# A gated linear unit that takes its columns as they lie in SBUF instead of in token order

## The chip, the cores and the metric

The kernel runs on one core of one Trainium2 chip. The metric is device time in microseconds (us) of one execution; the lower the better. The core has five engines that matter here: TensorE (PE in the profile, with its weight loads as PEld), VectorE (DVE), ScalarE (ACT), GpSimd (POOL) and the queue engine SyncE (SP), which issues most transfers. Each runs its own instructions in order and waits on semaphores for the others.

## The reference

One layer of a hybrid decoder over 2064 tokens (16 learned ones ahead of 2048) with 1024 features: a gated short convolution beside a diagonal state-space model (SSM), an output projection, then a gated MLP. The part that matters is the end of the SSM's branch, over 512 features:

```python
y = y.reshape(bsz, seq_len, D_SSM)
g = jax.nn.gelu(y)
out = g * jax.nn.sigmoid(g @ w_glu.astype(f32))
...
mixed = jnp.concatenate([rms_norm(conv_out, gain_conv_out[i]),
                         rms_norm(ssm_out, gain_ssm_out[i])], axis=-1)
h = h + mixed @ w_out[i].astype(h.dtype)
```

So g (512 features by 2064 tokens) is multiplied by a 512x512 weight, passed through a sigmoid, and multiplied onto itself. The columns of that product are independent of each other: any order of tokens gives the same result as long as the sigmoid meets its own column of g.

## The kernel before

Features lie on the 128 partitions, tokens on the free axis. All products are split in two parts to keep single precision: a matrix is written as hi + lo, and each output gets three matmuls, hi x hi, hi x lo and lo x hi (`product`, lines 128 to 142; the second operand is the one with 344 columns). Weights are loaded by SyncE (L119), their hi part is made by ScalarE and their lo part by VectorE (`parts`, L248 and L109), a few ahead of use by the class `Stream`. VectorE's two-operand operations all go through one helper, so that they all show as L109; one tells them apart by the names of the tiles.

The SSM works on chunks of 8 tokens and writes its result g to DRAM by position in the chunk. `load_glu` (L1012) reads it back as the tile `gt` of shape [128, 4, 8, 258]: feature group k, position j in the chunk (8), chunk c (258). Token number is 8c + j, so tokens that follow each other lie 258 elements apart in `gt`.

The tokens are handled in three blocks b of 688 columns, each in two halves c of 344 columns, which are 43 chunks of 8. Four steps use `gt`:

- `prep_glu` (L1016) makes the hi and lo parts of g for a block: `gh` on ScalarE (L1021), `gl` on VectorE (L1022, shown as L109). Six of each.
- `glu_block` (L1072) does the four products `pg` of a block, 24 matmuls each, with the weights `wh_g` and `wl_g`; then ScalarE's sigmoid into `sg` (L1079) and VectorE's gate product, `gt` times `sg`, in place (L1081, shown as L109). Twelve of each.
- `prep_ssm` (L1026) takes the RMS norm of the result: squares `sq_ms` (L164), sums on VectorE and, over partitions, on TensorE (`st_ms`, L188), the inverse root on GpSimd, its diagonal `dg_ms` (L203), a broadcast on TensorE (`sb_ms`, L208), the scaled `t_ms` (L1033), and its parts `h_ms` (L1038) and `l_ms`. It writes these in token order with the same helper `tokens`.
- `out_block` and `OutProj` multiply these by the output weight (`po`), adding the convolution's part, which `conv_part` has computed and kept for block 0 (`pk`, `kp`, L1064). The convolution's branch goes through the same steps as `prep_ssm` under the names `x_mc`, `sq_mc`, `st_mc`, `sb_mc`, `t_mc`, `h_mc` and `l_mc`, all unbroken.

The helper `tokens` turns a tile that lies in token order into a view by position: `(c j) -> j c`. Read or written through it, neighbours in the inner loop lie 8 elements apart.

Around the GLU the order of work is that in which the code is written, with `prep.step` letting the preparations for later blocks go forward between the products: `conv_part(0)`, `glu_block(0)`, `glu_block(1)`, `glu_block(2)`, `out_block(0)`, and so on. A tile scheduler then puts each engine's instructions in a fixed order; buffers of each pool go round, so that a load or a split waits for the last reader of its buffer.

Of the kernel before, what the change touches and what calls it, by code (L numbers as in the profile page):

```python
# [14 lines left out]
AF = mybir.ActivationFunctionType  # L15
ALU = mybir.AluOpType
# [6 lines left out]
NJ = 8  # L23
# [34 lines left out]
def layer_kernel(ctx, tc, xq, pk, w_in, w_glu, w_out, w_up, w_down, ssm_s, ssm_m, y):  # L58
    nc = tc.nc
    V, S, T, G = nc.vector, nc.scalar, nc.tensor, nc.gpsimd  # L60
# [34 lines left out]
    def mm_tile(name):  # L95
        return ps_mm.tile([P, 2, 512], F32, tag="mm", name=name)
# [5 lines left out]
    def f32(ap):  # L102
        return ap.bitcast(F32)

    def two(ap):
        return ap.rearrange("p (c t) -> p c t", c=2)

    def tt(out, a, b, op):
        V.tensor_tensor(out, a, b, op=op)  # L109

    def mul(out, a, b):
        tt(out, a, b, ALU.mult)
# [15 lines left out]
    def product(ps, w, rhs, nk, by_chunk=False, ks=None):  # L128

        hi, lo = w  # L130
        if by_chunk:
            for c, p in enumerate(ps):
                product([p], w, lambda k, _: rhs(k, c), nk)
            return
        for k in ks or range(nk):
            for c in range(len(ps)):
                xh, xl = rhs(k, c)
                T.matmul(ps[c], hi[:, k, :], xh, start=k == 0, stop=False)  # L138
                T.matmul(ps[c], hi[:, k, :], xl, start=False, stop=False)  # L139
            for c in range(len(ps)):  # L140
                xh, _ = rhs(k, c)
                T.matmul(ps[c], lo[:, k, :], xh, start=False, stop=k == nk - 1)  # L142

    def rhs_of(hs):
        return lambda k, c: (hs[c][k // 4][0][:, k % 4, :], hs[c][k // 4][1][:, k % 4, :])
# [4 lines left out]
    def hl_tile(n, name, pool=None, tag="xhl", bufs=8):  # L150
        return (pool or xf).tile([P, 4, QM], F32R, tag=tag, bufs=bufs, name=name)[:, :, :n]
# [812 lines left out]
    def until(res, n=2):  # L964
        while len(res) < n:
            prep.step()
# [38 lines left out]
    gt = a2.tile([P, 4, NJ, NC], F32, name="gt")  # L1005

    def tokens(a):

        names = "p k (c j) -> p k j c" if len(a.shape) == 3 else "p (c j) -> p j c"
        return a.rearrange(names, j=NJ)  # L1010
# [5 lines left out]
    def prep_glu(b, res, **kw):  # L1016
        for c in range(2):
            hi, lo = hl_tile(QL, f"gh_{b}_{c}", **kw), hl_tile(QL, f"gl_{b}_{c}", **kw)
            c0 = (2 * b + c) * 43
            src = gt[:, :, :, c0 : c0 + 43]  # L1020
            S.activation(tokens(hi), src, AF.Copy)  # L1021
            tt(tokens(lo), src, f32(tokens(hi)), ALU.subtract)  # L1022
            res.append(((hi, lo),))
            yield

# [20 lines left out]
    def ev_tile(name):  # L1046
        return a2.tile([P, B2], F32, tag="ev", bufs=3, name=name)
# [24 lines left out]
    def glu_block(b):  # L1072
        until(hg[b])
        rhs = rhs_of(hg[b])
        for m in range(4):
            ps = mm_tile(f"pg_{b}_{m}")
            product([ps[:, c, :QL] for c in range(2)], stream.take(), rhs, 4, by_chunk=m == 0)
            sg = ev_tile(f"sg_{b}_{m}")
            S.activation(two(sg), ps[:, :, :QL], AF.Sigmoid)  # L1079
            g = gt[:, m, :, b * 86 : b * 86 + 86]  # L1080
            mul(g, g, tokens(sg))  # L1081
            prep.step(2 if b else 1)

    hos = [[] for _ in range(3)]
    load_glu()
    prep.add(prep_glu(0, hg[0]), prep_glu(1, hg[1], **xh2))
    prep.lanes, slack = 1, True
    kept = conv_part(0)
    prep.lanes = 2
    until(hg[0])  # L1090
    prep.add(prep_glu(2, hg[2]))
    glu_block(0)
    until(hg[1])
    prep.add(prep_ssm(0, 0, hos[0]), prep_ssm(0, 1, hos[0]))
    prep.add(prep_conv(1, 0, hoc[1], **xh2), prep_conv(1, 1, hoc[1], **xh2))
    prep.lanes = 3
    glu_block(1)
    until(hg[2])
    glu_block(2)
    prep.lanes = 2  # L1100
    until(hos[0])
# [109 lines left out]
    for i in range(3):  # L1211
        c = C_FW + i * 44 + FT
# [183 lines left out]
    for b in range(3):  # L1396
# [4 lines left out]
        x, act, later = hf[b], {}, deque()  # L1401
# [248 lines left out]
```

## Time and profile before

| | |
|---|---|
| Time, median of 3 runs | 2223.89 us (2220.8 to 2225.02) |
| The profiled execution | 2220.69 us, its span 2218.9 us |
| TensorE busy over the span | 2121.5 us, 96% |
| VectorE busy | 1682.3 us, 76% |
| ScalarE busy | 1102.1 us, 50% |
| First and last start of a GLU matmul | 505.4 and 572.9 us |
| First matmul of the output projection behind it | 573.36 us |

The profile comes from one execution. Its rows give an instruction's engine, line, operation, the tiles it writes and reads, the shape, and a duration; in the order of time a bracket at the end of a row gives how long the engine had been idle before it, and whose work ended that. TensorE's matmuls are pipelined, so that the distance between starts, not the duration shown, is what one costs. The granted clock is TensorE's, as a share of its full speed.

### The profile page before, as it was taken

How to read it: one execution, taken by the hardware profiler on the slowest of the kernel's cores; microseconds unless marked ns; L12 is line 12 of the kernel's file. 1: busy time of each engine (PE TensorE's matmuls, PEld its weight loads, DVE VectorE, ACT ScalarE, POOL GpSimd, SP SyncE). 2: the span in 40 equal slices, each digit the busy share in tenths (PEclk: the TensorE clock that was granted, in tenths of full speed). 3: DMA queues.
4: the chain of work that ended last, by engine and by line, in shares of the span. 5: the costliest groups of instructions: out<-in, count | busy, mean ns of one | idle time of the engine just before them, and what ended most of it. 6: DMA issues, size and time to landing. Idle time of an engine off the chain costs nothing. (4 is left out here: it accounts for less than half of the span.)

```text
span 2218.9 us, 33122 instructions
## 1 busy us (share of the span) xinstructions
PE 2121.5 (96%) x13012; PEld 2061.5 (93%) x13012; DVE 1682.3 (76%) x2507; ACT 1102.1 (50%) x1651; POOL 151.4 (7%) x174
## 2 busy tenths in 40 slices
PE   7997999999899999999999899899999899999996
PEld 7997999998899999999999899899999899999996
DVE  8896499858956887686768869677868868667776
ACT  4135333337423555465556555455556555455555
POOL 0000000000000000100111010100111010110000
PEclk9998999999999999999999999999999999999998
DMA  7376544351576334624555262733555262653463
GB/s 241 108 219 164 145 149 150 108 178 53 162 233 202 134 105 120 142 80 112 129 130 130 91 169 76 211 107 87 139 128 141 82 170 62 158 120 95 101 170 113
DMA packets 170749, 300.28 MB, mean 135 GB/s; under 512 B 32416, under 2 KB 104800, under 8 KB 170464
## 3 DMA queue, kind: packets, MB, share of 16 engines
q1 hardware_dynamic: 149856, 246.41, 35.9%
q0 software_dynamic: 19584, 47.52, 12.6%
q10 hardware_dynamic: 1152, 4.23, 0.5%
q8 instruction: 102, 1.67, 0.3%
q14 instruction: 55, 0.45, 0.1%
HBM read 214.29 MB, written 83.82 MB: 134 GB/s over the span
## 5 line engine op out<-in xcount | busy, mean ns | idle before, releaser
L109 DVE TENSOR_TENSOR wl_up<-wr_up,wh_up 128x1024 fp32r<-128x1024 f32 x198 | 241.6, 1222 | 138.7 <-ACT wh_up L248 132.8
L138 PE MATMUL dn<-ah,wh_dn 128*128 128x344 f32 (+1 forms) x1024 | 327.8, 324 | 10.4 <-ACT ah L248 8.9
L139 PE MATMUL dn<-al,wh_dn 128*128 128x344 f32 (+1 forms) x1024 | 324.7, 320 | 0.4 <-DVE al L109 0.3
L248 ACT ACTIVATE wh_up<-wr_up 128x1024 fp32r<-128x1024 f32 x198 | 209.5, 1059 | 197.3 <-DVE wr_up L109 53.1
L1409 PE MATMUL xy<-h_t,wh_up 128*128 128x344 f32 (+1 forms) x792 | 263.9, 333 | 12.9 <-ACT z L1447 7.9
L1411 PE MATMUL xy<-h_t,wl_up 128*128 128x344 f32 (+1 forms) x792 | 254.0, 321 | 0.0
L1410 PE MATMUL xy<-l_t,wh_up 128*128 128x344 f32 (+1 forms) x792 | 253.7, 320 | 0.0
L142 PE MATMUL dn<-ah,wl_dn 128*128 128x344 f32 (+1 forms) x1024 | 247.3, 320 | 0.0
L138 PEld LDWEIGHTS dn<-ah,wh_dn 128*128 128x128 f32 x1024 | 193.6, 190 | 14.4 <-ACT ah L248 9.7
L1510 POOL DMA_DIRECT2D h_d<-ev x136 | 118.3, 870 | 1233.5 <-ACT ev L1506 1221.0
L139 PEld LDWEIGHTS dn<-al,wh_dn 128*128 128x128 f32 x1024 | 194.2, 190 | 1.8 <-DVE al L109 1.0
L1409 PE MATMUL xy<-h_b,wh_up 128*128 128x344 f32 (+1 forms) x528 | 176.5, 335 | 13.7 <-ACT z L1456 12.2
L1409 PEld LDWEIGHTS xy<-h_t,wh_up 128*128 128x128 f32 x792 | 149.8, 189 | 30.7 <-ACT z L1454 16.4
L142 PEld LDWEIGHTS dn<-ah,wl_dn 128*128 128x128 f32 x1024 | 178.1, 190 | 0.0
L1410 PE MATMUL xy<-l_b,wh_up 128*128 128x344 f32 (+1 forms) x528 | 169.9, 322 | 0.0
L1411 PE MATMUL xy<-h_b,wl_up 128*128 128x344 f32 (+1 forms) x528 | 168.6, 322 | 0.0
L248 ACT ACTIVATE wh_dn<-wr_dn 128x512 fp32r<-128x512 f32 (+1 forms) x144 | 85.5, 594 | 134.7 <-issue 52.5
L1410 PEld LDWEIGHTS xy<-l_t,wh_up 128*128 128x128 f32 x792 | 150.6, 190 | 0.0
L1411 PEld LDWEIGHTS xy<-h_t,wl_up 128*128 128x128 f32 x792 | 150.4, 190 | 0.0
L115 DVE SCALAR_TENSOR_TENSOR g<-z,pv,g 128x688 f32<-128x688 f32 (+1 forms) x132 | 122.3, 927 | 22.9 <-ACT g L1414 22.2
L109 DVE TENSOR_TENSOR wl_dn<-wr_dn,wh_dn 128x512 fp32r<-128x512 f32 (+1 forms) x144 | 92.5, 644 | 58.7 <-ACT wh_dn L248 57.4
L115 DVE SCALAR_TENSOR_TENSOR v<-z,pneg,v 128x688 f32<-128x688 f32 (+1 forms) x132 | 122.4, 928 | 9.4 <-ACT v L1414 8.1
(401 smaller groups left out, 5361.9 us busy)
## 6 DMA issues: line engine op xcount, KB each, us to landing
wr_up<-in_w_up SPq DMA_DIRECT2D x132, 512.0 KB, 5.4
h_d<-ev POOLq DMA_DIRECT2D x88, 344.0 KB, 6.8
wr_dn<-in_w_down SPq DMA_DIRECT2D x96, 256.0 KB, 2.7
wr_cw<-in_w_in SPq DMA_DIRECT2D x36, 512.0 KB, 4.5
h_d<-ev POOLq DMA_DIRECT2D x48, 336.0 KB, 6.6
x_c<-in_xq SPq DMA_DIRECT2D x16, 688.0 KB, 6.4
wr_dn<-in_w_down SPq DMA_DIRECT2D x48, 192.0 KB, 2.3
xr<-in_xq SPq DMA_DIRECT2D x24, 344.0 KB, 3.9
```

Of the source, the lines that this page charges most:

```text
L109: V.tensor_tensor(out, a, b, op=op)
L115: V.scalar_tensor_tensor(out=out, in0=a, scalar=s, in1=b, op0=ALU.mult, op1=ALU.add)
L138: T.matmul(ps[c], hi[:, k, :], xh, start=k == 0, stop=False)
L139: T.matmul(ps[c], hi[:, k, :], xl, start=False, stop=False)
L142: T.matmul(ps[c], lo[:, k, :], xh, start=False, stop=k == nk - 1)
L248: S.activation(hi, t, AF.Copy)
L1409: T.matmul(ps, hi[:, j, :], xh[:, j, :], start=start and j == 0, stop=False, **kw)
L1410: T.matmul(ps, hi[:, j, :], xl[:, j, :], start=False, stop=False, **kw)
L1411: T.matmul(ps, lo[:, j, :], xh[:, j, :], start=False, stop=j == 3, **kw)
L1510: G.dma_start(out=h_d[:, m, s0 : s0 + no], in_=ev, accum_op=ALU.add)
```

## The change

The GLU's product keeps its columns in the order of `gt`, position in the chunk first and then chunk (within each half of 344 columns). Three places follow from it:

- `gh` is written without `tokens`: ScalarE reads `gt` in runs of 43 as before and writes its 344 columns per feature group one after the other.
- `gl` is written, and `gh` read for it, in the same way by VectorE.
- `sg` therefore comes out in that order too. The gate product reads it unbroken, and walks `gt` by half, position and chunk (2 x 8 x 43) instead of by position and chunk (8 x 86).

The matmuls, the sigmoid and `prep_ssm` are the same. Every engine's instructions stand in the same order as before, with the same semaphores waited for; only the access patterns of these 24 instructions differ. Lines behind L1021 move down by one.

```diff
@@ prep_glu
             src = gt[:, :, :, c0 : c0 + 43]
-            S.activation(tokens(hi), src, AF.Copy)
-            tt(tokens(lo), src, f32(tokens(hi)), ALU.subtract)
+            hj, lj = (a.rearrange("p k (j c) -> p k j c", j=NJ) for a in (hi, lo))
+            S.activation(hj, src, AF.Copy)
+            tt(lj, src, f32(hj), ALU.subtract)
             res.append(((hi, lo),))
             yield
@@ glu_block
             S.activation(two(sg), ps[:, :, :QL], AF.Sigmoid)
-            g = gt[:, m, :, b * 86 : b * 86 + 86]
-            mul(g, g, tokens(sg))
+            g = gt[:, m, :, b * 86 : b * 86 + 86].rearrange("p j (c x) -> p c j x", c=2)
+            mul(g, g, two(sg).rearrange("p c (j x) -> p c j x", j=NJ))
             prep.step(2 if b else 1)
```

## The prediction

> **What bounds the kernel now.** First the profiled execution's own time, then the busy time by stretch around the gated linear unit (GLU), from the stretch before it to the first matmul of the output projection that follows it at 573.36 us.
>
> ```profile
> span 2218.9 us, 33122 instructions
> ```
>
> The run took 2220.69 us, 1.8 us more than this span; the median of the three runs shown is 2223.89. The columns below are TensorE matmul, its weight load, VectorE, ScalarE and GpSimd busy time, then TensorE's granted clock and the DMA share.
>
> ```profile
> 480.00:505.50 25.50, 25.50 (x162) 25.50 (x161) 5.75 (x5) 12.30 (x13) 0.00 (x0) 1.00 0.69 228
> 505.50:525.40 19.90, 17.32 (x99) 16.76 (x98) 19.61 (x13) 18.34 (x17) 0.00 (x0) 0.91 0.23 67
> 525.40:549.70 24.30, 21.91 (x122) 21.00 (x120) 18.91 (x34) 9.82 (x14) 3.19 (x3) 0.86 0.22 66
> 549.70:573.36 23.66, 18.69 (x107) 18.23 (x105) 21.09 (x25) 13.18 (x14) 1.16 (x1) 0.86 0.16 53
> ```
>
> Before the GLU, TensorE never pauses: 162 matmuls in 25.5 us, 0.157 us each, clock 1.00. In the three GLU stretches, one for each block of 688 columns, VectorE is busy 19.61 of 19.90, 18.91 of 24.30 and 21.09 of 23.66 us, TensorE has holes and its clock falls to 0.91 and 0.86. So here VectorE, fed by ScalarE, sets the pace, and TensorE, the bound of the program elsewhere, waits. The waits of TensorE from 495 to 600 us name the holes:
>
> ```profile
> PE st_mc L188 <- DVE sq_mc L109: 5.0, 1, 5.0
> PE st_ms L188 <- DVE sq_ms L109: 2.5, 2, 1.8
> PE pg L142 <- DVE wl_g L109: 2.2, 1, 2.2
> PE sb_ms L208 <- DVE dg_ms L203: 0.6, 1, 0.6
> PE pg L138 <- ACT sg L1079: 0.3, 1, 0.3
> ```
>
> Every one ends on a VectorE or ScalarE instruction that is not itself changed, but that stands in its queue behind the changed ones. TensorE's order of time shows what follows a hole:
>
> ```profile
> 505.68 0.32 PE L139 MATMUL pg<-gl,wh_g 128*128 128x344 f32 x1
> 508.24 0.66 PE L142 MATMUL pg<-gh,wl_g 128*128 128x344 f32 x1 [2.24 <-DVE wl_g L109]
> ...
> 511.51 0.32 PE L139 MATMUL pg<-gl,wh_g 128*128 128x344 f32 x1
> ...
> 535.40 1.29 PE L188 MATMUL st_ms<-ones,sq_ms 128*115 128x1 f32 x6 [1.79 <-DVE sq_ms L109]
> 536.55 0.64 PE L138 MATMUL pg<-gh,wh_g 128*128 128x344 f32 x1
> ...
> 542.95 0.32 PE L138 MATMUL pg<-gh,wh_g 128*128 128x344 f32 x1
> ...
> 582.00 0.73 PE L188 MATMUL st_ms<-ones,sq_ms 128*115 128x1 f32 x6 [0.66 <-DVE sq_ms L109]
> ```
>
> From 508.24 to 511.51 there are 11 matmuls: 3.27 us where 11 x 0.157 = 1.73 would do. From 536.55 to 542.95 there is one whole product, 24 matmuls: 6.40 us where 3.77 would do. A hole of about 2 us thus costs 1.5 to 2.6 us more in slow matmuls behind it.
>
> **What each changed instruction costs.** No instruction is added, removed or moved; on every engine and queue the order and the semaphores waited for are those of before. Only access patterns change, on 6 + 6 + 12 instructions. VectorE's groups from 330 to 720 us (last figures: busy us, mean ns), then ScalarE's:
>
> ```profile
> L109 DVE TENSOR_TENSOR gt<-gt,sg 128x688 f32<-128x688 f32 x12 | 18.2, 1517 | 2.5 <-ACT sg L1079 2.5
> L109 DVE TENSOR_TENSOR l_ms<-t_ms,h_ms 128x1376 fp32r<-128x1376 f32 x6 | 17.9, 3008 | 2.8 <-ACT h_ms L1038 2.6
> L109 DVE TENSOR_TENSOR gl<-gt,gh 128x1376 fp32r<-128x1376 f32 x6 | 17.5, 2924 | 10.6 <-ACT gh L1021 10.5
> ...
> L1033 DVE SCALAR_TENSOR_TENSOR t_ms<-gt,pv,rs_ms 128x344 f32<-128x344 f32 x24 | 12.5, 573 | 0.0
> L241 DVE SCALAR_TENSOR_TENSOR t_mc<-x_mc,pv,rs_mc 128x344 f32<-128x344 f32 x24 | 12.3, 584 | 0.0
> ...
> L109 DVE TENSOR_TENSOR l_mc<-t_mc,h_mc 128x1376 fp32r<-128x1376 f32 x6 | 9.4, 1601 | 0.1
> ...
> L109 DVE TENSOR_TENSOR xr<-kp,xr 128x688 f32<-128x688 f32 x8 | 7.1, 882 | 0.0
> ```
>
> ```profile
> L1021 ACT ACTIVATE gh<-gt 128x1376 fp32r<-128x1376 f32 x6 | 17.7, 2950 | 3.4 <-DMA gt<-g_d 3.4
> ...
> L1079 ACT ACTIVATE sg<-pg 128x688 f32<-128x688 f32 x12 | 8.9, 738 | 7.7 <-PE pg L142 7.7
> ...
> L164 ACT ACTIVATE sq_ms<-gt 128x1376 f32<-128x1376 f32 x6 | 8.1, 1366 | 4.8 <-DVE gt L109 3.5 <-DVE l_mc L109 1.2
> L248 ACT ACTIVATE h_mc<-t_mc 128x1376 fp32r<-128x1376 f32 x6 | 8.0, 1357 | 3.0 <-DVE t_mc L241 2.9
> ```
>
> *The high part (gh, ScalarE).* It reads gt in runs of 43 and writes every eighth element: 2.95 us. The square sq_ms has the very same read with an unbroken write: 1.366; h_mc, unbroken on both sides: 1.357. I take 1.37, saving 1.58 each, 9.5 us in all. The bounds lie 0.01 apart.
>
> *The low part (gl, VectorE).* Reads and writes at every eighth element: 2.924. l_mc, same size and operation, unbroken: 1.601. Runs of 43 on one operand remain, and t_ms, which has them on its source and its result, costs 0.573 where the unbroken t_mc costs 0.584: nothing. I take 1.60, saving 1.32 each, 7.9 us.
>
> *The gate product (gt, VectorE).* One operand, sg, was read at every eighth element: 1.517; afterwards it is unbroken, and gt's runs fall from 86 to 43. Lower end: xr<-kp, unbroken, 0.882. Upper end: as now, 1.517, if the pattern with one more dimension were slow. No row has exactly this form; t_ms with its runs of 43 is nearest, so I take 0.88, saving 0.64 each, 7.6 us.
>
> That is 15.5 us off VectorE and 9.5 off ScalarE; what counts is what they hold up. The GLU's matmuls read the same number of columns, unbroken, before and after: no change. prep_ssm's h_ms and l_ms keep the strided form (3.008).
>
> **Which holes close.** I go through TensorE's holes in time.
>
> 1. *508.24, waiting for wl_g.* ScalarE starts here:
>
> ```profile
> 498.39 2.92 ACT L1021 ACTIVATE gh<-gt 128x1376 fp32r<-128x1376 f32 x1 [3.36 <-DMA gt<-g_d]
> ```
>
> It then does a copy of 688 columns from PSUM (kp, as long as sg's 0.74) and the second gh; afterwards this ends near 498.39 + 1.37 + 0.74 + 1.37 = 501.9. VectorE does the second gl until 503.5 and wl_g (512 columns, so less than the 0.88 of xr's 688) until 504.4 at the latest, before TensorE comes for it at 505.7. Hole gone: 2.24. Slow matmuls behind it gone: 3.27 - 1.73 = 1.54.
>
> 2. *The 0.3 us wait for the sigmoid.* ScalarE's queue up to sg loses 6 x 1.58 us, TensorE arrives only 3.8 us earlier: gone, 0.3.
>
> 3. *535.40, waiting for sq_ms.* The chain from the end of block 0's last product: sg 0.74, gate product 0.88, two squares on ScalarE 2 x 1.37, sg 0.74, gate product 0.88, the last sum of 344 columns (at most t_mc's 0.58), and by my estimate 0.6 for hand-overs and the weight split ahead of sg: 7.2 us. TensorE meanwhile has two products, 48 x 0.157 = 7.5 us, and the first st_ms; the second took 1.15 us (535.40 to 536.55) at the slow clock, so 1.15 x 3.77/6.40 = 0.68 without it. That is 8.2, so TensorE comes 1.0 us after the sums and the hole goes: 1.79. Behind it go 6.40 - 3.77 = 2.63 of slow matmuls and the 1.15 - 0.68 = 0.47 of the slow st_ms.
>
> 4. *The 0.6 us wait for dg_ms.* One gate product stands ahead of dg_ms in VectorE's queue: 0.64 less, hole gone, 0.6.
>
> 5. *The 5.0 us wait for sq_mc* stays but for one gate product:
>
> ```profile
> 559.49 1.49 DVE L109 TENSOR_TENSOR gt<-gt,sg 128x688 f32<-128x688 f32 x1
> ```
>
> Its chain runs from the end of block 1's last product through sg, two h_ms on ScalarE (of gh's present form, 2.95 each), l_ms (3.01), then this product, t_mc and the sums. The h_ms and l_ms, unchanged, carry it. 0.6 saved, 4.4 left, and the slow matmuls behind it left.
>
> 6. *582.00, waiting for sq_ms.* Block 2's last gate product stands ahead on VectorE: 0.64 of 0.66, say 0.6.
>
> Sum: 2.24 + 1.54 + 0.3 + 1.79 + 2.63 + 0.47 + 0.6 + 0.6 + 0.6 = 10.8 us. After that TensorE is again the bound, and everything behind it, the loads of weights too, which are started by freed buffers, moves forward by the same amount. From 2220.69 this gives 2209.9; from the median, 2223.89 - 10.8 = 2213.1 us.
>
> The slow matmuls are the term with the least footing. The Trainium skill, "TensorE: Matmul & The Clock Gate", Part 1 (the HAM clock gate), says that the clock is halved after an idle window of about 3.4 us, counted by a free-running window, and comes back after about as long a busy one; by that rule holes of 2.24 and 1.79 us would be too short to slow anything. The rows above differ: the matmuls behind both holes are slow, and nowhere in the dense stretch ahead, so I count the slow clock to the holes.
>
> **The rivals.**
> - *The slow clock stays.* If the slow runs at 508 and 536 us do not belong to the holes but come from VectorE-paced work in any case, the 1.54, 2.63 and 0.47 stay: 10.8 - 4.6 = 6.2 saved, 2217.7 us. For it: the holes are short. Against: clock 1.00 without holes. The Trainium skill's rule just named leads there. Chance 0.10.
> - *The gate product stays at 1.5 us.* Then holes 4, 5 and 6 stay (1.8), and hole 3's chain is 2 x 0.64 longer than its 7.2, 0.3 over the 8.2, a hole that I take for too short to slow the clock: 10.8 - 2.1 = 8.7 saved, 2215.2. Against: t_ms. Chance 0.07.
> - *Slower.* Each run of 43 costs VectorE a start of r in the gate product, which has 16 where it had 8. With 0.88 + 16r each, r = 0.04 us merely undoes the gain. At r = 0.15 it takes 3.3 us, 1.8 more than now: it would hit hole 3 twice and holes 4, 5 and 6 once, +9.0, against the 4.1 us that gh and gl still bring in holes 1 and 2: 4.9 slower, 2228.8. Break-even is near r = 0.1. Against: eight runs in t_ms cost nothing measurable. Chance 0.03.
> - *Nothing reaches the end*: the weights' loads take over as the last to arrive. Against: during the GLU the DMA share is 0.16 to 0.23. 2223.9, chance 0.03.
>
> **How the numbers follow.** My forecast has 0.77, and its own spread: hole 5 and the slow stretch behind it may move by 2 us either way, and the three runs of before differ by 4.2 us, so that about 0.2%, 4.4 us, is what a measurement tells from no change. Range 2207.5 to 2217.7: from 10.8 + 2 + some 3 for the runs at the low end, to the first rival at the high end, taking in the second. Faster by over 0.2%: the forecast, the second rival and most of the first, 0.90; within: 0.07; slower: 0.03.
>
> **What would show it.** Right: gh near 1.37, gl near 1.60, the gate product near 0.88 us; no wait of TensorE for wl_g, and none for sq_ms at the first st_ms; the 5 us wait for sq_mc still there at 4 to 4.5 us; clock 1.00 in the first GLU block; the first po matmul near 563 us instead of 573.36. Wrong: the changed instructions keep their times (the stride was not the cost), or the clock row of the first two blocks still shows 0.9 with the holes gone (first rival), or a hole of several us opens at another place, such as a weight load, that now comes last.

## The result, and the profile after

In five runs each the changed kernel takes 2210.14 us (2206.98 to 2215.93), the one before 2222.83 us (2220.80 to 2225.02): ratio 0.9948, 95% interval 0.9931 to 0.9964. On another chip it was 2206.96 against 2220.66 us, ratio 0.9940, interval 0.9926 to 0.9954. So it is faster by 12.7 and 13.7 us, where 10.8 were forecast; the first interval comes to 8.0 to 15.3 us, so that the forecast lies inside it. The profiled execution took 2206.98 us, the shortest of the five, with a span of 2205.2.

The changed instructions in the profile after, first VectorE's and then ScalarE's groups of the same stretch, 330 to 720 us:

```profile
L109 DVE TENSOR_TENSOR gt<-gt,sg 128x688 f32<-128x688 f32 x12 | 10.5, 871 | 4.3 <-ACT sg L1080 4.3
L109 DVE TENSOR_TENSOR gl<-gt,gh 128x1376 fp32r<-128x1376 f32 x6 | 9.5, 1590 | 8.8 <-ACT gh L1022 8.8
```

```profile
L1022 ACT ACTIVATE gh<-gt 128x1376 fp32r<-128x1376 f32 x6 | 8.2, 1362 | 3.5 <-DMA gt<-g_d 3.5
```

1.52 us has become 0.87, 2.92 has become 1.59 and 2.95 has become 1.36: within 0.01 us of the values taken. The halving of the gate product's runs to 43 elements costs nothing.

TensorE's waits from 495 to 700 us, after:

```profile
PE st_mc L188 <- DVE sq_mc L109: 4.3, 1, 4.3
PE po L138 <- DVE xr L109: 1.8, 1, 1.8
PE po L138 <- ACT h_ms L1039: 1.2, 1, 1.2
...
```

Holes 1, 2, 3, 4 and 6 are no longer among them; hole 5 stands at 4.3 us. The same three stretches of the GLU by their events (block 0; block 1 up to the first matmul of block 2; block 2 up to the first po), after:

```profile
505.55:520.75 15.20, 15.20 (x98) 15.20 (x97) 10.82 (x13) 9.89 (x14) 0.00 (x0) 1.00 0.37 116
520.75:539.44 18.69, 18.69 (x122) 17.96 (x121) 14.32 (x31) 10.06 (x14) 2.95 (x3) 1.00 0.19 57
539.44:562.67 23.23, 18.90 (x107) 18.45 (x105) 18.63 (x25) 13.18 (x14) 1.17 (x1) 0.85 0.19 58
```

In the first two, TensorE is busy throughout at clock 1.00, and VectorE for 10.82 of 15.20 and 14.32 of 18.69 us: the pace has gone over to TensorE. The third still has its hole and a clock of 0.85. TensorE's order of time, after, at the places that were holes 1, 3, 4, 5 and 6:

```profile
505.56 0.32 PE L138 MATMUL pg<-gh,wh_g 128*128 128x344 f32 x1
...
528.35 1.27 PE L188 MATMUL st_ms<-ones,sq_ms 128*115 128x1 f32 x12
...
536.57 0.82 PE L208 MATMUL sb_ms<-dg_ms,ones 115*128 115x344 f32 x2
...
554.02 1.29 PE L188 MATMUL st_mc<-ones,sq_mc 128*115 128x1 f32 x6 [4.33 <-DVE sq_mc L109]
...
562.67 0.58 PE L138 MATMUL po<-h_ms,wh_o 128*128 128x344 f32 x1
...
570.64 0.73 PE L188 MATMUL st_ms<-ones,sq_ms 128*115 128x1 f32 x6
```

The two st_ms, a row of six each with 1.79 us between them before, now stand in one row of twelve. The distance from the first product matmul (505.52 before, 505.56 after) to the first po is the measure that I use below: 67.83 us before, 57.11 after. I call it the stretch.

### The profile page after: what moved, and what is told of

Read it like the earlier page. It is cut to its first block, busy times and chain, and to the rows that moved or that the text cites. A ratio compares the mean times of both kernels' runs of the same rounds, so it can differ in the third digit from the quotient of the medians.

```text
span 2205.2 us, 33122 instructions
## 1 busy us (share of the span) xinstructions
PE 2116.5 (96%) x13012; PEld 2058.6 (93%) x13012; DVE 1666.8 (76%) x2507; ACT 1093.6 (50%) x1651; POOL 151.5 (7%) x174
## 3 DMA queue, kind: packets, MB, share of 16 engines
q0 software_dynamic: 19584, 47.52, 12.7%
## 5 line engine op out<-in xcount | busy, mean ns | idle before, releaser
L1410 PE MATMUL xy<-h_b,wh_up 128*128 128x344 f32 (+1 forms) x528 | 176.4, 335 | 12.3 <-ACT z L1457 10.8
```

The lines of the kernel that those rows point to most:

```text
L1410: T.matmul(ps, hi[:, j, :], xh[:, j, :], start=start and j == 0, stop=False, **kw)
```

## The experiments

All of them start from the changed kernel, and none moves an instruction unless that is said. TensorE reached the first GLU matmul between 505.0 and 509.0 us in them, so stretches are compared, not times of day. Each stretch comes from one profiled execution.

A stretch also depends on where the halved clock behind hole 5 lies. That clock lasts 6.8 us in every profile with a hole 5 of 4 us or more, but it begins earlier or later in the hole: 4.96 us of it lie behind the hole in the changed kernel's first profile, 5.81 in its second, 6.41 with gh strided and 6.85 with the parts alone. At half the clock TensorE loses about half of that, so a stretch moves by up to 0.9 us with it.

Six of the experiments were single executions: the parts alone took 2212.59 us, the gate product alone 2210.46, gh strided 2215.68 and gl twice 2216.09, beside 2217.78 for one execution of the kernel before; gl strided took 2210.93 and t_ms by token 2200.21, beside a median of 2220.66. The five runs of the changed kernel lie up to 9 us apart, so single times decide nothing here.

**The parts alone.** The gate product goes back to its old pattern:

```diff
-            g = gt[:, m, :, b * 86 : b * 86 + 86].rearrange("p j (c x) -> p c j x", c=2)
-            mul(g, g, two(sg).rearrange("p c (j x) -> p c j x", j=NJ))
+            g = gt[:, m, :, b * 86 : b * 86 + 86]
+            mul(g, g, tokens(sg))
```

> Only gh and gl take the new order; the gate product keeps its old pattern, so it pairs each sigmoid with another token's g (same work, other values). My theory: gh 1.36 and gl 1.59 us, the product back at 1.5; holes 1 and 2 closed (4.1 us), hole 3 closed or at most 0.5 us and its slow matmuls gone, holes 4 (0.6), 5 (5.0) and 6 (0.7) as before the change. First po matmul at 564.5 to 565.5 us (573.36 before, 562.67 with the whole change). Rival 'the slow clock has nothing to do with the holes': the clock is halved near 508 and 535 us although the holes are gone, first po near 568. Rival 'the gate product is all covered': first po at 562.7.

The waits of TensorE from 495 to 580 us:

```profile
PE st_mc L188 <- DVE sq_mc L109: 5.3, 2, 4.9
PE st_ms L188 <- DVE sq_ms L109: 0.6, 1, 0.6
PE sb_ms L208 <- DVE dg_ms L203: 0.6, 1, 0.6
```

TensorE's order of time shows which of the holes these are:

```profile
530.07 1.51 PE L188 MATMUL st_ms<-ones,sq_ms 128*115 128x1 f32 x12
536.12 0.73 PE L188 MATMUL st_mc<-ones,sq_mc 128*115 128x1 f32 x6 [0.47 <-DVE sq_mc L109]
...
539.88 0.82 PE L208 MATMUL sb_ms<-dg_ms,ones 115*128 115x344 f32 x2 [0.59 <-DVE dg_ms L203]
...
557.87 1.27 PE L188 MATMUL st_mc<-ones,sq_mc 128*115 128x1 f32 x6 [4.88 <-DVE sq_mc L109]
...
576.00 0.73 PE L188 MATMUL st_ms<-ones,sq_ms 128*115 128x1 f32 x6 [0.65 <-DVE sq_ms L109]
```

The product is at 1.50 us, the stretch 60.09 us: 7.7 of the 10.7 us. Holes 1 and 3 are closed (the two st_ms stand in one row of twelve) and no halved clock stands in their places; a wait of 0.47 us has opened at the st_mc behind hole 3. Holes 4, 5 and 6 are as they were: the wait of 0.6 us for sq_ms in the list is hole 6, at 576.0 us. TensorE started its first product 1.7 us later than expected, so that the first po came at 567.4; taken as a stretch the expectation (59 to 60) holds to 0.2 us. Both rivals fall: the clock does not halve near 508 and 535 us once the holes are gone, and the gate product is not covered. It still costs 3.0 us of the stretch, of which 0.9 are the place of the halved clock behind hole 5.

**The gate product alone.** gh and gl go back to the old pattern:

```diff
-            S.activation(hj, src, AF.Copy)
-            tt(lj, src, f32(hj), ALU.subtract)
+            S.activation(tokens(hi), src, AF.Copy)
+            tt(tokens(lo), src, f32(tokens(hi)), ALU.subtract)
```

> Only the gate product takes the new pattern; gh and gl stay strided, so the product pairs each sigmoid with another token's g (same work, other values). My theory: hole 1 stays (2.2 us, wl_g) with slow matmuls behind it, hole 2 stays; hole 3's chain has two products of 0.88 and the hole closes with its slow matmuls; hole 4 closes, hole 5 at 4.4, hole 6 closes. First po matmul at 567 to 568 us. Rival 'the gate product is all covered': first po at 573. Rival 'the slow clock is independent': as before at all three places, first po at 570 to 571.

```profile
PE st_mc L188 <- DVE sq_mc L109: 4.3, 1, 4.3
PE pg L142 <- DVE wl_g L109: 2.2, 1, 2.2
PE pg L138 <- ACT sg L1079: 0.3, 1, 0.3
```

Holes 1 and 2 stay to the tenth, and behind hole 1 the clock is halved for 3.4 us from 507.8; holes 3, 4 and 6 are gone. The stretch is 61.37 us, 6.5 saved. The two parts alone save 7.7 + 6.5 = 14.2 us, together 10.7: hole 3, with the slow matmuls behind it, is closed by either, so it counts in both.

**ScalarE alone slow.** Only gh is written at every eighth element:

```diff
-            S.activation(hj, src, AF.Copy)
+            S.activation(tokens(hi), src, AF.Copy)
```

> As the changed kernel, but gh alone is written at every eighth element, while gl subtracts as if it lay unbroken (same work, wrong values): ScalarE alone is slow again. My theory: gh 2.95, gl 1.59, product 0.87; ScalarE's queue holds wh_g and kp late: a hole of 1.2 to 1.5 us at wl_g, another of up to 2 us where a PSUM buffer waits for kp; hole 3 closed. First po at 566 to 568. Rival 'only VectorE's time counts': no new hole, first po at 562.7 to 563.

```profile
PE st_mc L188 <- DVE sq_mc L109: 4.3, 1, 4.3
PE pg L138 <- ACT sg L1080: 1.8, 1, 1.8
PE pg L138 <- ACT kp L1065: 1.2, 1, 1.2
PE pg L142 <- DVE wl_g L109: 0.8, 1, 0.8
```

gh takes 2.93 us, gl 1.59. Three holes open: at wl_g, smaller than the 1.2 to 1.5 us expected, at kp as expected, and at the sigmoid, which was not expected (1.8 us, with 3.4 us of halved clock from 524.0). The stretch is 63.78 us, more than the 60.4 to 62.4 to which the expected times come. ScalarE's slowness alone gives back 6.7 of the 10.7 us (0.7 of them by the place of the halved clock behind hole 5), so 'only VectorE's time counts' falls.

**VectorE alone slow.** Only gl is written at every eighth element; it reads unbroken:

```diff
-            tt(lj, src, f32(hj), ALU.subtract)
+            tt(tokens(lo), src, f32(hj), ALU.subtract)
```

> As the changed kernel, but gl alone is written at every eighth element, while it reads unbroken (same work, wrong values): VectorE alone is slow again, order of instructions unchanged. My theory: a strided write alone makes gl 2.9 us, as a strided read alone made the product 1.5; ScalarE being fast, hole 1 is 0 to 0.5 us and the st_ms hole 0 to 0.6, without slow matmuls; from first pg to first po 57.3 to 58.6 us (57.1 with the whole change, 67.8 before). Rival 'VectorE alone made the holes': hole 1 near 1 us, st_ms hole over 1 us with slow matmuls, 60 us or more. Rival 'only reads cost': gl stays at 1.6, 57.1 us.

Its group from 495 to 620 us:

```profile
L109 DVE TENSOR_TENSOR gl<-gt,gh 128x1376 fp32r<-128x1376 f32 x6 | 17.4, 2926 | 8.3 <-ACT gh L1022 8.3
```

One strided side is enough for the full price, 2.926 us, where before two strided sides cost 2.924. The stretch is 57.59 us, 0.5 more than with the whole change (0.15 more than in its second profile), and the list of TensorE's waits has nothing but hole 5 (4.4 us) between 495 and 580 us; at wl_g it pauses for 0.12 us. So hole 1, which I had described as VectorE's queue fed by ScalarE, is 2.2 us with both parts slow, 0.8 with gh alone slow and 0.1 with gl alone slow: ScalarE's gh counted for more, and VectorE had slack once it got its work in time. TensorE came 1.0 us later to its first product here, but that hides nothing of a hole 1, because ScalarE came later too: the first gh starts 7.14 us ahead of TensorE's first product before, 6.97 after, 7.13 here and 7.31 with gh strided.

**gl twice, unbroken.** To tell time from stride:

```diff
             tt(lj, src, f32(hj), ALU.subtract)
+            tt(lj, src, f32(hj), ALU.subtract)
```

> The changed kernel with gl computed twice, unbroken: VectorE spends 3.1 us on each pair, slightly more than the 2.92 of the strided one, with no strided access. My theory (queue time alone): with ScalarE fast, the hole at wl_g is 0.5 to 0.9 us, another near st_ms of 0.4 to 1.1 us, hole 5 at 4.3; first po at 563.5 to 565. Rival 'strided access slows other engines beside it': nothing beyond 562.7 to 563, as no access is strided.

Inconclusive. With six more instructions the scheduler put the gate products ahead of the later gl, and st_mc of the fourth norm 13 GLU matmuls later. The stretch is 58.73 us, 1.6 more than with the whole change, with hole 5 at 4.8 and no other listed. It speaks for time on the queue without any stride, but its order of work is not that of the others.

**t_ms by token.** Hole 5's chain runs through h_ms and l_ms, each strided. Here VectorE pays the stride once, in t_ms, and both parts are unbroken:

```diff
-        t = half_tile(QL, f"t_ms{q}", tag="sq", bufs=2).rearrange("p k (j c) -> p k j c", j=NJ)
+        t = half_tile(QL, f"t_ms{q}", tag="sq", bufs=2)
...
-                out=t[:, k], in0=src[:, k], scalar=col(C_GS + k), ...
+                out=tokens(t)[:, k], in0=src[:, k], scalar=col(C_GS + k), ...
...
-        S.activation(tokens(hi), t, AF.Copy)
-        tt(tokens(lo), t, f32(tokens(hi)), ALU.subtract)
+        parts(t, hi, lo)
```

> The changed kernel, and t_ms is now written in token order by VectorE (every eighth element, 4 x 344 elements), so that h_ms and l_ms behind it are unbroken. My theory: t_ms 0.9 instead of 0.57 us, h_ms 1.36 instead of 2.98, l_ms 1.59 instead of 3.01; hole 5 (sq_mc, 4.3 us) falls to 1 to 2.5 us, and from first pg to first po 53 to 55.5 us instead of 57.1. Rival 'hole 5 does not hang on h_ms and l_ms': it stays at 4.3.

Its groups on VectorE and ScalarE from 495 to 620 us, and the one wait of TensorE from 495 to 580 us:

```profile
L1034 DVE SCALAR_TENSOR_TENSOR t_ms<-gt,pv,rs_ms 128x344 f32<-128x344 f32 x16 | 12.2, 881 | 0.0
...
L109 DVE TENSOR_TENSOR l_ms<-t_ms,h_ms 128x1376 fp32r<-128x1376 f32 x4 | 6.4, 1590 | 0.0
...
L248 ACT ACTIVATE h_ms<-t_ms 128x1376 fp32r<-128x1376 f32 x4 | 5.4, 1362 | 4.6 <-DVE t_ms L1034 4.6
```

```profile
PE st_mc L188 <- DVE sq_mc L109: 1.3, 1, 1.3
```

As expected in every price; hole 5 falls from 4.3 to 1.3 us, the stretch to 53.44 us, and the 1.8 us wait for xr behind it falls to 0.2. Four t_ms cost 1.2 us more and one l_ms 1.4 less, so VectorE gains little; it is ScalarE's two h_ms, 1.6 us less each, that shorten the chain. What is left of hole 5 is VectorE's: in the changed kernel it waits 1.30 us for h_ms ahead of its two l_ms, here it works without a pause from t_ms to sq_mc.

Timed on another chip:

> The kernel with t_ms in token order, timed. My theory: its first profile had 53.4 us from first pg to first po against 57.1 and no hole of 1.8 us at po behind it, so some 4 + 2 us, and the slow matmuls behind those holes, off the changed kernel's time: 2199 to 2203 us, ratio to before 0.990 to 0.992. Rival 'the first time was a lucky clock': 2205 or more.

2202.86 us against 2219.74, ratio 0.9930, interval 0.9914 to 0.9946, stretch 53.47: at the upper end of the times expected and a little behind the ratio.

**st_mc later.** Nothing gets faster; TensorE is only given its other work first:

```diff
+        if name == "mc3":
+            for _ in range(4):
+                yield
         return (yield from inv_rms_of(s, 4 * P * len(groups), n, name, out))
```

> The changed kernel with the matmuls st_mc of the fourth norm emitted four steps later, which puts them behind the last GLU product instead of inside the third of block 2; VectorE's and ScalarE's order changes slightly with it. My theory: hole 5 (4.3 us) and the slow matmuls behind it (6.8 us at half clock, so up to 3.4 us) go, and no other hole over 1 us opens: from first pg to first po 49.5 to 51.5 us instead of 57.1; the whole 5 to 8 us faster than the changed kernel. Rival 'VectorE is the pace there in any case': a new hole of 3 us or more opens at the first po, for l_ms or a weight split; no gain.

The waits of TensorE from 495 to 620 us:

```profile
PE sb_ms L211 <- DVE dg_ms L206: 1.7, 1, 1.7
PE pg L142 <- DVE wl_g L109: 1.6, 1, 1.6
PE sb_ms L211 <- ACT h_mc L251: 1.6, 1, 1.6
```

Hole 5 and the halved clock behind it are gone and the stretch is 51.80 us, a little over the range. But a new wait of 1.6 us (for wl_g) opens inside it, against the expectation that none over 1 us would, and two of 1.6 and 1.7 us in the output projection. The time is 2203.45 us, against 2206.96 of the changed kernel on the same chip: 3.5 us less, not 5 to 8. Part of what was won was given back in the new holes. The second profile of the changed kernel was taken beside it:

> The changed kernel again, beside the other three on one chip: 0.9931 to 0.9964 of before, from first pg to first po 57.1 us, holes as in its first profile. If slow matmuls belong to holes, the clock is full from the first pg to hole 5 here too; the rival 'clock by chance' would show a halved stretch there in this second profile.

Its stretch is 57.44 us, with the same holes, and the clock is full from the first product to hole 5.

**Both.** t_ms by token, and st_mc one step later, behind ten more matmuls:

> The same, with st_mc of the fourth norm one step later, which puts it behind the third product of block 2, ten matmuls (1.6 us) later than hole 5's 1.3 us. My theory: no hole over 0.5 us and no halved clock from the first pg to the first po: 50.0 to 52.0 us instead of 53.4, and 1 to 3 us off the whole. Rival 'short holes do not matter to the clock': as far as 52.1 us and only 1.3 us off the whole.

The stretch is 50.09 us, without halved clock and without a hole in it. But that is flattered by its measure:

```profile
559.04 0.31 PE L138 MATMUL po<-h_ms,wh_o 128*128 128x344 f32 x1
560.78 0.84 PE L211 MATMUL sb_mc<-dg_mc,ones 115*128 115x344 f32 x2 [1.43 <-DVE dg_mc L206]
561.21 0.58 PE L139 MATMUL po<-l_ms,wh_o 128*128 128x344 f32 x1
```

The first po has gone ahead of sb_mc, which waits 1.4 us for dg_mc right behind the end of the stretch; with t_ms by token alone sb_mc stands ahead of the first po. To the second po it is 52.26 us, where t_ms by token has 53.86 and 53.89: 1.6 us less, not 3.4. The time is 2201.72 us against 2219.74, ratio 0.9917, interval 0.9901 to 0.9932: the lowest median of the timed kernels, 1.1 us under t_ms by token alone, which is less than their runs differ. The whole time thus can't tell the expectation (1 to 3 us) from its rival (1.3 us); the full clock speaks against the rival.

## Why the prediction was right

By its own terms, from events of TensorE in both profiles:

| Place | forecast, us | measured, us | from |
|---|---|---|---|
| holes 1 and 2 and slow matmuls | 4.1 | 4.54 | first pg to first pg of block 1: 19.73, now 15.19 |
| hole 3, slow st_ms and matmuls | 4.9 | 5.10 | from there to 542.95, now 533.35 |
| hole 4 | 0.6 | 0.63 | from there to 546.80, now 536.57 |
| part of hole 5 | 0.6 | 0.64 | from there to 564.89, now 554.02 |
| slow matmuls behind hole 5 | 0 | -0.18 | from there to the first po |
| hole 6 | 0.6 | 0.67 | from there to st_ms at 582.00, now 570.64 |
| sum | 10.8 | 11.40 | |

The prices of the three instructions, the five holes that close and the one that stays were as the steps had them. (The low end of the range, 2207.5 us, takes 3.6 us for the runs where the text says some 3; nothing hangs on it.) The -0.18 us behind hole 5 is the place of the halved clock again: 4.57 us of it lie behind the hole before, 4.96 after. Two things were not as the steps had them:

*Who held hole 1.* I wrote that VectorE, fed by ScalarE, sets the pace. The experiments with one engine slow at a time show that ScalarE's gh counted for more there, and that VectorE's gl costs little unless gh is slow too. Of VectorE's two savings it is the gate product's that shows by itself. The forecast of the closed hole was right because both parts got faster.

*What came on top.* Profile against profile the gain is 13.7 us, 2.3 more than at st_ms. I had assumed that the clock behind the later holes stays as it was. Before, the hole of 1.87 us at 606.5 us has 3.4 us of halved clock behind it, and after, the hole of 1.76 us at 595.0 has none; halved for 3.4 us, TensorE loses 1.7. The stretches before:

```profile
508.00:511.40 3.40, 3.16 (x11) 3.17 (x12) 3.40 (x3) 3.40 (x4) 0.00 (x0) 0.50 0.27 82
535.30:542.10 6.80, 6.70 (x25) 6.73 (x26) 4.70 (x10) 0.76 (x1) 2.02 (x2) 0.50 0.27 80
562.60:569.40 6.80, 4.51 (x18) 4.54 (x19) 5.63 (x8) 1.46 (x2) 1.16 (x1) 0.50 0.45 144
607.00:610.40 3.40, 3.40 (x14) 3.40 (x13) 3.40 (x5) 0.65 (x1) 0.00 (x0) 0.50 1.02 301
```

and after:

```profile
552.10:558.90 6.80, 4.88 (x19) 4.91 (x20) 4.73 (x7) 1.82 (x2) 1.17 (x1) 0.50 0.56 177
590.00:600.00 10.00, 8.24 (x52) 7.99 (x53) 10.00 (x10) 4.27 (x4) 0.00 (x0) 1.00 0.74 253
```

This is luck, and it does not stay: the changed kernel has a halved stretch at 743.3 us that the kernel before has not, and by 760 us the gain between the same matmuls is back at 11.6 us. In the MLP it goes on between 10.4 and 13.8 us as halved stretches fall differently. Between 600 and 2190 us they come to 37.5 us before and 34.1 after, one piece of 3.4 and so up to 1.7 us less, which is most of the 2.3. The second profile of the changed kernel has 44.4 us of them there and a span of 2210.8 us, 5.6 longer than the first; half of the difference would be 5.1. So the forecast is to be held against the 11.4 us of the table; what a profile gains or loses on top hangs mostly on where the halved clock fell. No cause of the last 0.6 us was looked for.

The rival that the slow clock is independent of the holes is out: nine profiles with hole 1 closed show full clock at its place and at that of hole 3, and the kernel with the gate product alone, in which hole 1 stays, shows it halved. How often holes of the size of 1 and 3 bring a halved clock is not shown: that the sum's 4.6 us of slow matmuls came out rests on one profile of the kernel before, in which both did; hole 1 is seen once more, with the gate product alone, and there too. The rival that the gate product stays slow is out by its 0.871 us; forced back, it costs 3.0 us of the stretch, where 2.1 were worked out, and the difference of 0.9 us is the place of the halved clock behind hole 5. The slower rival needed runs of 43 to cost; they cost nothing. The rival that nothing reaches the end is out by the time.

## What to carry to other kernels

When an intermediate is consumed only elementwise and by columns that don't depend on each other, keep it in the order in which its source lies, and reorder once, at the last step that needs it, by one strided write ahead of all that read the result; t_ms by token did that and took 3.7 us off the stretch. Price such a change by the holes of the engine that sets the end, and by all engines ahead of each hole: here ScalarE and VectorE together lost 25 us of work, and TensorE gained 11. Where a hole is left, look whether TensorE's own order puts the waiting instruction ahead of work that is ready; but moving it hands the wait on to what is next in line.

## What the runs showed of the hardware

- On VectorE one strided operand, read or write, is enough for the whole price of the stride. At every eighth 4-byte element it pays 0.94 us more per thousand elements for a read (product, 1.517 against 0.871 us for 688), 0.97 for a write (gl, 2.926 against 1.590 for 1376) and the same for both at once (2.924). ScalarE pays 1.15 for a write (2.950 against 1.362); a strided read alone was not measured on it. Runs of 43 elements cost nothing (the product 0.871, the unbroken xr 0.882).
- A read of gt in runs of 43 and a write at every eighth element in one three-operand operation (t_ms) went from 0.572 to 0.881 us for 344 elements: 0.90 per thousand, close to the other two.
- TensorE's halved clock comes in pieces of 3.4 us or a multiple, mostly 3.4 or 6.8 us (10.2 at 1402.7 us in the kernel with both), and within a profile the pieces begin whole multiples of 3.41 us apart: before, at 508.0, 535.3, 562.6 and 607.0 us, with 8, 8 and 13 times 3.41 between them. Of the holes listed in this document, none of 0.8 us or less had it, both of 2.2 us had 3.4 us, and every one of 4 us or more had 6.8 us of it. Those of 1.2 to 1.9 us had it in some profiles and not in others at the very same place, and the grid shows why. The windows of that grid with the wait for xr, before and after (the clock in them is full, what counts is the next window):

```profile
603.59:607.00 3.41, 1.54 (x10) 1.29 (x9) 3.41 (x5) 2.41 (x2) 0.00 (x0) 1.00 0.42 128
593.11:596.52 3.41, 1.65 (x11) 1.54 (x11) 3.41 (x5) 1.96 (x2) 0.00 (x0) 1.00 0.31 76
```

Before, TensorE is idle for 1.87 us of this window, and the next is halved; after, for 1.76, and the next is not. For this wait the four profiles with a halved piece have 1.84 to 1.90 us in one window (before, gate product alone, gl twice, gl strided), the four without have at most 1.76, 1.46, 1.62 and 1.17 (after, its second profile, parts alone, gh strided), in some because the hole lies across two windows. Over the twelve profiles, from 250 to 2150 us, one can count for each window at full clock how long TensorE had nothing but one-column matmuls (st_ms, st_mc and the like) or nothing at all: all 81 windows with 1.9 us or more of that were followed by a halved one, none of 6409 with less than 1.6, and 18 of the 28 between. The hole of 1.3 us with t_ms by token fits in: with the row st_mc right behind it, it makes 1.9 us in one window, and a halved piece follows in both profiles of that kernel. The Trainium skill, "TensorE: Matmul & The Clock Gate", Part 1 (the HAM clock gate), tells of a window of about 3.4 us that runs freely; the grid agrees with that. Its statement that it takes an idle window of that length differs from these runs, where 1.9 us of a window were enough each time.

- Some of the spread between runs of one kernel goes with this: the five runs of the changed kernel had mean clocks of 0.983, 0.982, 0.983, 0.980 and 0.982 at 2206.98, 2210.14, 2207.73, 2215.93 and 2212.58 us.
